# Last pair of expert columns exchanged, dense blocks first in the output sum, its products kept in written order

## The chip, the cores and the metric

The kernel runs on one core of one Trainium2 chip. The metric is the device time of one execution in microseconds; the median of the runs of the kernel before is 2418.31 us. TensorE is called PE (PEld is its loading of weights), VectorE DVE, ScalarE ACT, GpSimd POOL and SyncE SP. Everything is float32 at the edges; many products run in pieces of the type fp32r, which the kernel makes itself by splitting a number into a rounded part ("hi") and the rest ("lo").

## The reference

A layer of a diffusion backbone for 256 latent and 256 context tokens of width 2048: a modulated norm, one input projection, a bidirectional mLSTM and a differential attention, a gated merge, an output projection, and then the part that matters here, a retrieval of experts (PEER):

```python
def peer(h, w_pq, sub_keys, expert_u, expert_v):
    ...
    top_s, pos = lax.top_k(cand_s, P_TOPK)
    idx = jnp.take_along_axis(cand_i, pos, axis=-1)
    g = jax.nn.softmax(top_s, axis=-1)
    ...
        act = jax.nn.gelu(jnp.einsum('td,ted->te', hx, expert_u[ix]).astype(jnp.float32), approximate=False)
        return jnp.einsum('te,ted->td', (gx * act).astype(h.dtype), expert_v[ix])
```

Each of the 256 tokens picks 8 x 16 of 16384 experts; an expert is a row of `expert_u` (2048 numbers, gives its activation) and a row of `expert_v` (2048 numbers, added to the output with gate times activation).

## The kernel before, in words

**The sum over expert columns.** The kernel does not gather `expert_u`; it multiplies all of it. The 16384 experts are 128 columns (i1) of 128 experts. The loop over `i1` at the end of `build` takes two columns at a time ("a pair"). `u_pair` (L80, `mp_`) makes 4 x 16 products for a pair from four pieces of `expert_u`, which the generator `pieces` names in order, `load` (L104) brings in by SP's queue into three buffers, and ACT (L120) and DVE or POOL (L123) split into hi and lo. DVE sums the halves (L1507), ACT takes the gelu (L1508), and ACT's queue stores the activations to the table `ag_dram` in HBM (L1512). Beside this loop `plan` runs in small steps: it finds the top experts, builds the gates of every expert and token (`gate_map`, stored to `ag_dram` by `map_out`, L1235, on SP's queue), and sorts the experts that are in use into lists (`lists`).

**Dense and listed columns.** The last two columns, 126 and 127 (N_LIST = 126), are not listed: their activations stay on chip in `act_tail`, are multiplied by `gate_tail` (L1513), and all their 128 experts enter the output sum ("dense"). For the other 126 columns `lists` makes 99 blocks of 128 experts: 37 blocks for both token tiles (BOTH), 14 for one tile (7 and 7), and 48 for 32 tokens each, of which four make one group. `idxV` and `idxG` hold the row numbers of a block in `expert_v` and `ag_dram`.

**The output sum.** `ITEMS` sets its order: a block, or a group of four. `stage_rows` brings a block's 128 rows of `expert_v` (128x2048, 1 MB) into `vraw`: a dense block by SP's queue, a listed one by an indirect gather on POOL's queue (L1429, `gather`). `vraw` tiles hold two blocks, and there are four of them, which share their place with the tiles `gates` of `gate_map`. `stage_gates` gathers a block's gates and activations (`ag`, 128x512 for BOTH, else 128x256) from `ag_dram`, so it needs all stores of the table. `weights_of` multiplies the two (L1466; L1463 for a group) and, but for groups, splits the product into the halves l (or d for a dense block; L1450 on ACT, L1451 on DVE). `split` does the same for rows (L1442 on ACT, L1444 on DVE). The products go to eight banks of PSUM, `out_acc[t][c]` (v00 to v13: token tile t, 512 columns c). `v_part` (L1525) makes three products (hi-hi, lo-hi, hi-lo) for each bank of a half, with all 128 columns of the array: 24 for a BOTH or dense block, 12 for a block of one tile, 1104 in all. `v_groups` (L1539) multiplies a group unsplit: block j of the four writes 32 output partitions from 32 j, so that it uses 32 columns of the array:

```python
        for c in range(4):
            for j, (raw, ins) in enumerate(parts):
                mm(out_acc[t][c][32 * j:32 * j + 32, :], lhsT=ins[t], rhs=raw[:, c * 512:(c + 1) * 512],
```

These 16 products appear as 32 matmuls in the trace (384 for twelve groups). `next_item` and `fetch_gates` fetch ahead: eight blocks of rows, 8 and 4 `ag` tiles.

**What sets the order.** A framework puts instructions of each engine in an order that it finds by its own estimate of times, unless `tc.keep_in_program_order` (as in `mp_`) keeps an instruction in the order in which the code issues it. In the kernel before the products of `u_pair` are kept so, those of the output sum aren't. All gathers of POOL are kept in their order. After the first N_FIRST = 5 items an `If` (L1562) handles blocks for which there was no room in the lists (none here); behind it `fin` tiles (four of 1 MB: the final norm's weight, a modulation row, the residual) are loaded.

Of the kernel before, what the change touches and what calls it, by code (L numbers as in the profile page):

```python
# [25 lines left out]
OP = mybir.AluOpType  # L26
# [4 lines left out]
P = 128  # L31
# [21 lines left out]
N_LIST = P - 2  # L53
CAPS = (6,) * 8 + (7, 7, 37)
# [5 lines left out]
BOTH, DENSE = 10, 11  # L60


def spread(*groups):
    return [x for _, _, x in sorted(((i + 0.5) / len(g), j, x) for j, g in enumerate(groups) for i, x in enumerate(g))]

ITEMS = [[(BOTH, i)] for i in range(3)] + [[(DENSE, i)] for i in range(N_LIST, P)] + spread(
    [[(4 * t + j, i) for j in range(4)] for i in range(6) for t in range(2)],
    [[(BOTH, i)] for i in range(3, CAPS[BOTH])],  # L70
    [[(8 + n % 2, n // 2)] for n in range(11)]) + [[(9, 5)], [(8, 6)], [(9, 6)]]


def build(tc, a, dump=None):
    nc = tc.nc
    mm = nc.tensor.matmul


    def mp_(*args, **kw):
        tc.keep_in_program_order(mm(*args, **kw))  # L80
# [45 lines left out]
    def pieces():  # L126
        first = [BLOCKS.index(b) for b in FIRST]
        for kp in range(8):
            for i in first:
                yield a["w_in"][i, kp]  # L130
        for i in range(len(BLOCKS)):
            for kp in range(8 if i not in first else 0):
                yield a["w_in"][i, kp]
        for blk in range(4):
            for kp in range(8):
                yield a["w_pb" if kp < 4 else "w_pa"][blk, kp % 4]
        for n in ("w_out", "w_pq"):
            for i in range(32):
                yield a[n][i // 8, i % 8]
        for i in range(2 * P):  # L140
            yield a["expert_u"][i // 2, i % 2]

    ahead = []
    todo = pieces()
# [263 lines left out]
    for k in range(KT):  # L408
# [7 lines left out]
        for kp in range(4):  # L416
            w = load(a["w_mod1"][k, kp], stx, MOD_BUFS)
            for k4 in range(4):
                mm(ps[32 * k4:32 * k4 + 32, 0:T], lhsT=s1[:, 4 * kp + k4, :], rhs=w[:, k4 * T:(k4 + 1) * T],
                   start=kp == 0, stop=kp == 3, skip_group_check=True)  # L420
# [670 lines left out]
    act_tail = tkr.tile([P, P - N_LIST, T], F32, name="act_tail")  # L1091
    gate_tail = tkr.tile([P, P - N_LIST, T], F32, name="gate_tail")
# [314 lines left out]
    n = P - N_LIST + 1  # L1407
# [61 lines left out]

    FIRST_OF = [sum(len(x) for x in ITEMS[:n]) for n in range(len(ITEMS) + 1)]  # L1470
    rows_in = []
    gates_in = []
    staged = [0, 0]


    AG = 8, 4
    USES = [[sum(k != DENSE and len(TILES[k]) == w for k, _ in x) for w in (1, 2)] for x in ITEMS]

    def fetch_gates(n):
        while staged[1] < len(ITEMS) and all(sum(u[w] for u in USES[n:staged[1] + 1]) <= AG[w] for w in range(2)):  # L1480
            gates_in.append([stage_gates(*b) for b in ITEMS[staged[1]]])
            staged[1] += 1

# [9 lines left out]

    back.append(plan())
    pump(1)
    for i1 in range(0, P, 2):
        if i1 == N_LIST:

            drain()
            vst = tc.alloc_tile_pool(name="vst", bufs=1, side="right", reuse_waits="tile")  # L1500
        pss = u_pair(i1, 1.05)
        if i1 == N_LIST:
            (raw0, ins0), = next_item(0)
            hl0 = split(raw0[:, 0:1024])
        act = act_tail if i1 == N_LIST else gm.tile([P, 2, T], F32, name="act", tag="act", bufs=2)
        for e, ps in enumerate(pss):
            nc.vector.reduce_sum(act[:, e], ps.rearrange("p s t -> p t s"), axis=AX.X)  # L1507
        nc.scalar.activation(act, act, AF.Gelu)  # L1508
        if i1 < N_LIST:
            rows = ag_dram[i1 * P:(i1 + 2) * P].rearrange("(i p) (t c) -> p i t c", p=P, t=2)  # L1510
            for t in range(2):
                nc.scalar.dma_start(rows[:, :, t, 0:P], act[:, :, t * P:(t + 1) * P])  # L1512
    nc.vector.tensor_tensor(act_tail, act_tail, gate_tail, op=OP.mult)  # L1513
    psS.release()
    psG.release()
    h2p.release()
# [3 lines left out]
    out_acc = [[psV.tile([P, 512], F32, name=f"v{t}{c}") for c in range(4)] for t in range(2)]  # L1520

    def v_part(hl, ins, t, hf_, first=False, last=False, cs=(0, 1)):
        for i, (sa, sb) in enumerate(PASS):
            for c in cs:
                mm(out_acc[t][hf_ * 2 + c], lhsT=ins[sa], rhs=hl[sb][:, c * 512:(c + 1) * 512],  # L1525
                   start=first and i == 0, stop=last and i == 2, skip_group_check=True)

    def v_block(n, raw, ins, hl=None):
        for hf_ in range(2):
# [6 lines left out]
    def v_groups(t, parts):  # L1536
        for c in range(4):
            for j, (raw, ins) in enumerate(parts):
                mm(out_acc[t][c][32 * j:32 * j + 32, :], lhsT=ins[t], rhs=raw[:, c * 512:(c + 1) * 512],  # L1539
                   start=False, stop=False, skip_group_check=True)  # L1540

    def v_item(n):
        parts = next_item(n)
# [3 lines left out]
            v_block(n, *parts[0])  # L1547

    v_block(0, raw0, ins0, hl0)
    N_FIRST = 3 + P - N_LIST  # L1550
    for n in range(1, N_FIRST):
        v_item(n)

# [8 lines left out]
    with tc.If(rest > 0):  # L1562
        with tc.For_i(0, N_LIST, 1) as i:
            col_ = av.tile([P, 1], F32, name="ocol", bufs=1)
            nc.sync.dma_start(col_, over_dram[:, bass.ds(i, 1)])
            for t in range(2):
                ag = av.tile([P, 2 * P], F32, name="oag", bufs=1)
                nc.sync.dma_start(ag, ag_dram[bass.ds(i * P, P), 2 * t * P:2 * (t + 1) * P])
                w = av.tile([P, P], F32, name="ow", bufs=1)
                nc.vector.scalar_tensor_tensor(w, ag[:, 0:P], col_, ag[:, P:2 * P], op0=OP.mult, op1=OP.mult)  # L1570
                ins = halves(w, P, "o", 1, av)
                for c in range(4):
                    raw = av.tile([P, 512], F32, name="oraw", bufs=1)
                    nc.sync.dma_start(raw, FULL[bass.ds(i * P, P), c * 512:(c + 1) * 512])
                    hl = halves(raw, 512, "r", 1, av)
# [131 lines left out]
```

## Time and profile before

| | |
|---|---|
| runs | 2418.4, 2416.95, 2418.31 us; median 2418.31 |
| profiled execution | 2422.88 us, of which the span from the first to the last instruction is 2421.2 us |
| PE busy | 2326.2 us (96% of the span) |
| DVE, ACT, POOL busy | 1542.8, 1140.5, 894.1 us |
| moved | 571.04 MB, mean 236 GB/s |
| granted clock of TensorE | 0.985 of full speed in the mean |

The span has some 2023 us up to the last product of the expert columns, and then the output sum and the end. PE is busy nearly all the time, but a busy PE need not be at its peak: a matmul with 32 of 128 columns of the array counts as much as one with all of them. So the time of each kind of product is read from the time between starts in a stretch, and the DMA's share and rate beside it.

### The profile page before, as it was taken

How to read it: one execution, taken by the hardware profiler on the slowest of the kernel's cores; microseconds unless marked ns; L12 is line 12 of the kernel's file. 1: busy time of each engine (PE TensorE's matmuls, PEld its weight loads, DVE VectorE, ACT ScalarE, POOL GpSimd, SP SyncE). 2: the span in 40 equal slices, each digit the busy share in tenths (PEclk: the TensorE clock that was granted, in tenths of full speed). 3: DMA queues.
4: the chain of work that ended last, by engine and by line, in shares of the span. 5: the costliest groups of instructions: out<-in, count | busy, mean ns of one | idle time of the engine just before them, and what ended most of it. 6: DMA issues, size and time to landing. Idle time of an engine off the chain costs nothing. (4 is left out here: it accounts for less than half of the span.)

```text
span 2421.2 us, 38180 instructions
## 1 busy us (share of the span) xinstructions
PE 2326.2 (96%) x14434; PEld 1971.9 (81%) x14434; DVE 1542.8 (64%) x2808; ACT 1140.5 (47%) x1913; POOL 894.1 (37%) x910
## 2 busy tenths in 40 slices
PE   6999999999999999989999989999999998999996
PEld 3679989998898999779888878887889887665663
DVE  3357874669766768564788976675665545444445
ACT  3231322244548544444446766794358643333333
POOL 2132201236533200000145564672237524656552
PEclk9999999999999999999999999999999999999998
DMA  9969855875536788755565567788765568998884
GB/s 383 347 201 321 318 192 180 287 214 165 153 115 189 239 281 272 244 197 184 165 200 173 174 183 222 218 219 238 216 191 170 163 213 293 385 368 321 344 337 158
DMA packets 235899, 571.04 MB, mean 236 GB/s; under 512 B 85138, under 2 KB 118723, under 8 KB 221248
## 3 DMA queue, kind: packets, MB, share of 16 engines
q1 hardware_dynamic: 153744, 338.29, 43.7%
q0 software_dynamic: 47120, 212.72, 24.7%
q10 hardware_dynamic: 34848, 17.57, 2.5%
q8 instruction: 113, 1.85, 0.3%
q14 instruction: 74, 0.61, 0.1%
HBM read 524.33 MB, written 38.93 MB: 233 GB/s over the span
## 5 line engine op out<-in xcount | busy, mean ns | idle before, releaser
L120 ACT CAST hi<-raw 128x1024 fp32r<-128x1024 f32 x528 | 552.4, 1048 | 794.0 <-PE acc L275 257.3
L123 DVE TENSOR_TENSOR lo<-raw,hi 128x1024 fp32r<-128x1024 f32 x465 | 590.2, 1272 | 328.8 <-ACT hi L120 323.0
L80 PE MATMUL s<-h,hi 128*128 128x512 f32 x2048 | 740.4, 403 | 1.0 <-ACT hi L120 1.0
L80 PE MATMUL s<-h,lo 128*128 128x256 f32 x2048 | 579.5, 283 | 20.8 <-POOL lo L123 11.5
L80 PEld LDWEIGHTS s<-h,hi 128*128 128x128 f32 x2048 | 388.2, 190 | 88.7 <-ACT hi L120 1.7
L275 PE MATMUL acc<-hL,hi 128*128 128x256 f32 x2048 | 420.5, 285 | 0.0
L80 PEld LDWEIGHTS s<-h,lo 128*128 128x128 f32 x2048 | 390.0, 190 | 28.7 <-POOL lo L123 14.2
L275 PEld LDWEIGHTS acc<-hL,hi 128*128 128x128 f32 x2048 | 339.4, 192 | 4.2 <-issue 3.9
L275 PE MATMUL acc<-hL,lo 128*128 128x256 f32 x1024 | 291.3, 285 | 3.9 <-DVE lo L123 3.9
L123 POOL TENSOR_TENSOR lo<-raw,hi 128x1024 fp32r<-128x1024 f32 x63 | 152.4, 2419 | 275.5 <-ACT hi L120 261.7
L1525 PE MATMUL v<-hi,l 128*128 128x512 f32 x704 | 197.7, 398 | 8.7 <-ACT l L1450 8.6
L1444 DVE TENSOR_TENSOR lo<-vraw,hi 128x1024 fp32r<-128x1024 f32 x106 | 129.2, 1234 | 118.1 <-ACT hi L1442 116.3
L275 PEld LDWEIGHTS acc<-hL,lo 128*128 128x128 f32 x1024 | 196.2, 192 | 5.9 <-DVE lo L123 4.9
L104 POOL DMA_DIRECT2D raw<-w_mod x128 | 67.9, 531 | 305.9 <-DVE raw L508 284.7
L508 DVE SCALAR_TENSOR_TENSOR raw<-raw,cr 128x1024 f32<-128x1024 f32 x128 | 154.9, 1221 | 36.9 <-DMA raw<-w_mod 21.4
L1223 POOL TENSOR_SCALAR o<-iota,i1T,gT 128x128 f32<-128x128 f32 x128 | 140.8, 1107 | 94.5 <-PE g L80 50.3
L1442 ACT CAST hi<-vraw 128x1024 fp32r<-128x1024 f32 x106 | 108.7, 1046 | 138.4 <-PE v L1525 134.0
L1525 PEld LDWEIGHTS v<-hi,l 128*128 128x128 f32 x704 | 132.5, 190 | 49.5 <-issue 10.6
L1429 POOL DMA_INDIRECT vraw<-expert_v,idxV x99 | 105.7, 1068 | 105.4 <-DVE l L1451 31.5
L275 PE MATMUL acc<-hC,hi 128*128 128x256 f32 x512 | 134.0, 283 | 0.0
L1507 DVE TENSOR_REDUCE act<-s 128x256 f32<-128x512 f32 x126 | 86.4, 686 | 58.1 <-PE s L80 52.8
L1429 POOL DMA_INDIRECT ag<-ag_dram,idxG x99 | 102.6, 1036 | 47.3 <-issue 26.2
(406 smaller groups left out, 3971.9 us busy)
## 6 DMA issues: line engine op xcount, KB each, us to landing
raw<-expert_u SPq DMA_DIRECT2D x256, 512.0 KB, 4.1
raw<-w_in SPq DMA_DIRECT2D x176, 512.0 KB, 4.5
raw<-w_mod POOLq DMA_DIRECT2D x128, 512.0 KB, 5.3
raw<-w_mod SPq DMA_DIRECT2D x64, 512.0 KB, 7.4
raw<-w_out SPq DMA_DIRECT2D x32, 512.0 KB, 3.6
raw<-w_pq SPq DMA_DIRECT2D x32, 512.0 KB, 3.3
ag_dram<-gates SPq DMA_DIRECT2D x32, 512.0 KB, 6.7
ag_dram<-act ACTq DMA_DIRECT2D x126, 128.0 KB, 4.0
```

The lines of the kernel that those rows point to most:

```text
L80: tc.keep_in_program_order(mm(*args, **kw))
L104: d = queue.dma_start(r, src)
L120: nc.scalar.copy(h, r)
L123: (nc.vector if shared[0] else nc.gpsimd).tensor_tensor(l, r, h.bitcast(F32), op=OP.subtract)
L275: mm(acc[c][:, g * T:(g + 1) * T], lhsT=hl[sb][:, k2 * 512 + c * P:k2 * 512 + (c + 1) * P], rhs=rhs(sa, g, k), start=first and k2 == 0 and ...
L508: product = nc.vector.scalar_tensor_tensor(r, r, 1.0, cr, op0=OP.mult, op1=OP.mult, accum_out=part[:, h, i:i + 1])
L1223: (nc.gpsimd if i % 2 else nc.vector).tensor_scalar(o2[:, i, 0:width], iota[:, 0:width], cols[:, i:i + 1], factor[:, i:i + 1], op0=OP.is_e ...
L1429: tc.keep_in_program_order(nc.gpsimd.indirect_dma_start(out=out, out_offset=None, in_=src, in_offset=bass.IndirectOffsetOnAxis(ap=idx[:, b ...
L1442: nc.scalar.copy(h, raw)
L1444: nc.vector.tensor_tensor(l, raw, h.bitcast(F32), op=OP.subtract)
L1507: nc.vector.reduce_sum(act[:, e], ps.rearrange("p s t -> p t s"), axis=AX.X)
L1525: mm(out_acc[t][hf_ * 2 + c], lhsT=ins[sa], rhs=hl[sb][:, c * 512:(c + 1) * 512], start=first and i == 0, stop=last and i == 2, skip_group ...
```

## The change

Three things change. `PAIRS` exchanges the last two pairs of columns: 122, then 126 (the dense pair), then 124. The pieces of `expert_u` follow this order, and `act_tail` is multiplied by `gate_tail` as soon as the dense pair's gelu is done. `ITEMS` puts the two dense blocks first, then two BOTH blocks; the third goes to the spread list. The gates for items behind the first are now fetched only when the second item is called for (`fetch_gates`), since they need the stores of pair 124; the `If` stands behind four items. And the products of `v_part` and `v_groups` go through `mp_`, so that PE has them in the order in which the code issues them.

```diff
-ITEMS = [[(BOTH, i)] for i in range(3)] + [[(DENSE, i)] for i in range(N_LIST, P)] + spread(
+ITEMS = [[(DENSE, i)] for i in range(N_LIST, P)] + [[(BOTH, i)] for i in range(2)] + spread(
     [[(4 * t + j, i) for j in range(4)] for i in range(6) for t in range(2)],
-    [[(BOTH, i)] for i in range(3, CAPS[BOTH])],
+    [[(BOTH, i)] for i in range(2, CAPS[BOTH])],
     [[(8 + n % 2, n // 2)] for n in range(11)]) + [[(9, 5)], [(8, 6)], [(9, 6)]]
+
+PAIRS = list(range(0, P - 4, 2)) + [P - 2, P - 4]
...
-        for i in range(2 * P):
-            yield a["expert_u"][i // 2, i % 2]
+        for i in PAIRS:
+            for j in range(4):
+                yield a["expert_u"][i + j // 2, j % 2]
...
-        while staged[1] < len(ITEMS) and all(sum(u[w] for u in USES[n:staged[1] + 1]) <= AG[w] for w in range(2)):
+        while staged[1] < (len(ITEMS) if n else 1) and all(sum(u[w] for u in USES[n:staged[1] + 1]) <= AG[w] for w in range(2)):
...
-    for i1 in range(0, P, 2):
-        if i1 == N_LIST:
+    for i1 in PAIRS:
+        if i1 == PAIRS[-1]:
...
-        if i1 == N_LIST:
+        if i1 == PAIRS[-1]:
             (raw0, ins0), = next_item(0)
...
-    nc.vector.tensor_tensor(act_tail, act_tail, gate_tail, op=OP.mult)
+        else:
+            nc.vector.tensor_tensor(act_tail, act_tail, gate_tail, op=OP.mult)
...
-                mm(out_acc[t][hf_ * 2 + c], lhsT=ins[sa], rhs=hl[sb][:, c * 512:(c + 1) * 512],
-                   start=first and i == 0, stop=last and i == 2, skip_group_check=True)
+                mp_(out_acc[t][hf_ * 2 + c], lhsT=ins[sa], rhs=hl[sb][:, c * 512:(c + 1) * 512],
+                    start=first and i == 0, stop=last and i == 2, skip_group_check=True)
...
-                mm(out_acc[t][c][32 * j:32 * j + 32, :], lhsT=ins[t], rhs=raw[:, c * 512:(c + 1) * 512],
-                   start=False, stop=False, skip_group_check=True)
+                mp_(out_acc[t][c][32 * j:32 * j + 32, :], lhsT=ins[t], rhs=raw[:, c * 512:(c + 1) * 512],
+                    start=False, stop=False, skip_group_check=True)
...
-    N_FIRST = 3 + P - N_LIST
+    N_FIRST = 4
```

What this does to the order of instructions, at three places. In the rows the line comes first (the changed program has other line numbers: L82 is `mp_`, L106 `load`, L1238 `map_out`, L1426 `stage_rows`), then the operation, the tile written and the tiles read.

**PE, the head of the output sum.** Before:

```order
L80 MATMUL s_20497<-h2_15_10177,lo_20479 128x256
L1525 MATMUL v00_20581<-hi_20567,l0_20557 128x512
L1525 MATMUL v01_20582<-hi_20567,l0_20557 128x512
L1525 MATMUL v00_20581<-lo_20569,l0_20557 128x512
L1525 MATMUL v01_20582<-lo_20569,l0_20557 128x512
L1525 MATMUL v02_20583<-hi_20601,l0_20557 128x512
```

Now:

```order
L82 MATMUL s_20495<-h2_15_10177,lo_20477 128x256
L82 MATMUL v00_20556<-hi_20540,d0_20536 128x512
L82 MATMUL v01_20557<-hi_20540,d0_20536 128x512
L82 MATMUL v00_20556<-lo_20542,d0_20536 128x512
L82 MATMUL v01_20557<-lo_20542,d0_20536 128x512
L82 MATMUL v00_20556<-hi_20540,d1_20537 128x512
```

The first products before read l, made from a gathered `ag` tile of a listed block; now they read d, made from `act_tail`, and 48 of them stand ahead of the first that reads an l.

**PE, the second group of four blocks** (w32 are the four blocks' weights, in order of j). Before:

```order
L1539 MATMUL v10_20585<-vraw_21009,w32_21183 32x512
L1539 MATMUL v11_20586<-vraw_21009,w32_21183 32x512
L1525 MATMUL v02_20583<-lo_21166,l0_21138 128x512
...
L1525 MATMUL v13_20588<-hi_21164,l1_21145 128x512
L1539 MATMUL v12_20587<-vraw_21009,w32_21183 32x512
L1539 MATMUL v13_20588<-vraw_21009,w32_21183 32x512
L1539 MATMUL v10_20585<-vraw_21009,w32_21185 32x512
L1539 MATMUL v11_20586<-vraw_21009,w32_21185 32x512
L1539 MATMUL v12_20587<-vraw_21009,w32_21185 32x512
```

Now:

```order
L82 MATMUL v13_20563<-hi_21118,l1_21099 128x512
L82 MATMUL v10_20560<-vraw_20960,w32_21134 32x512
L82 MATMUL v10_20560<-vraw_21009,w32_21136 32x512
L82 MATMUL v10_20560<-vraw_21009,w32_21138 32x512
L82 MATMUL v10_20560<-vraw_21012,w32_21140 32x512
L82 MATMUL v11_20561<-vraw_20960,w32_21134 32x512
L82 MATMUL v11_20561<-vraw_21009,w32_21136 32x512
```

Before, the banks changed and the block stayed, and eight products of another block stood in between; now the four blocks come one after the other for each bank, and the group stands together. Eleven of the twelve groups stood torn by eight products and, for the most part, block by block, like this one; the first had one product early, and its other fifteen stood as the code has them.

**SP, the rows of the dense blocks.** Before, behind all but one of the loads of `expert_u`:

```order
L104 DMA raw_20421<-expert_u 128x1024
L104 DMA raw_20453<-expert_u 128x1024
L1423 DMA vraw_20533<-expert_v 128x2048
L1423 DMA vraw_20536<-expert_v 128x2048
L104 DMA raw_20475<-expert_u 128x1024
```

Now, among the stores of the gates:

```order
L106 DMA raw_16797<-expert_u 128x1024
L1238 DMA ag_dram_83<-gates_15751 128x16x64
L1426 DMA vraw_20528<-expert_v 128x2048 x2
L106 DMA raw_16839<-expert_u 128x1024
L106 DMA raw_16883<-expert_u 128x1024
L1238 DMA ag_dram_83<-gates_15751 128x16x64
```

Both 1 MB loads moved ahead by some 130 places of SP's queue, behind the fifth of the eight stores of the third quarter of the gates. On POOL, three rows of listed blocks are gathered ahead of the first `ag` tile instead of four, and nine `ag` tiles instead of eleven ahead of the rows of the first group.

## Rows read from the trace of the kernel before

**Rows 1.** The page: the span.

```profile
span 2421.2 us, 38180 instructions
```

**Rows 2.** Busy time by stretch: us, five engines, granted clock, DMA share, GB/s.

```profile
2008.00:2023.00 15.00, 14.68 (x84) 12.51 (x82) 7.71 (x8) 6.07 (x7) 5.33 (x5) 1.00 1.02 420
2031.00:2037.00 6.00, 5.72 (x15) 4.53 (x16) 3.00 (x13) 1.52 (x6) 4.76 (x5) 0.55 0.60 174
2070.00:2100.00 30.00, 30.00 (x136) 18.32 (x129) 13.80 (x27) 10.08 (x15) 19.41 (x19) 1.00 1.02 421
2100.00:2150.00 50.00, 50.00 (x200) 32.93 (x199) 22.75 (x46) 16.73 (x25) 32.34 (x31) 1.00 0.98 389
2150.00:2200.00 50.00, 50.00 (x206) 31.07 (x205) 24.13 (x47) 19.21 (x28) 28.38 (x27) 1.00 0.86 331
```

**Rows 3.** Timeline of PE: start, us, line, tiles, count, [idle before <- releaser].

```profile
2022.41 0.28 PE L80 MATMUL s<-h,lo 128*128 128x256 f32 x1
2031.28 1.22 PE L1525 MATMUL v<-hi,l 128*128 128x512 f32 x2 [8.60 <-ACT l L1450]
...
2036.48 0.62 PE L1525 MATMUL v<-hi,l 128*128 128x512 f32 x2
...
2050.42 1.10 PE L1525 MATMUL v<-hi,d 128*128 128x512 f32 x4
2061.89 1.17 PE L1525 MATMUL v<-hi,l 128*128 128x512 f32 x4
2065.79 1.04 PE L1539 MATMUL v<-vraw,w 128*32 128x512 f32 x2
...
2401.94 0.63 PE L1525 MATMUL v<-hi,l 128*128 128x512 f32 x1
```

**Rows 4.** Timelines of POOL, ACT and DVE at the head of the output sum.

```profile
2013.28 1.13 POOL L1429 DMA_INDIRECT vraw<-expert_v,idxV  x1 [0.30 <-issue]
2027.22 0.95 POOL L1429 DMA_INDIRECT ag<-ag_dram,idxG  x1 [12.81 <-SPq L1562]
2028.47 0.95 POOL L1429 DMA_INDIRECT ag<-ag_dram,idxG  x1 [0.30 <-issue]
2012.90 0.94 ACTq L1512 DMA_DIRECT2D ag_dram<-act  x2
2023.56 0.62 ACT L1508 ACTIVATE act_tail<-act_tail 128x512 f32<-128x512 f32 x1
2022.72 0.69 DVE L1507 TENSOR_REDUCE act_tail<-s 128x256 f32<-128x512 f32 x1 [0.64 <-PE s L80]
```

**Rows 5.** The tile `ag_dram`, 1990 to 2060 us: all its DMAs.

```profile
DMA to landing us min/median/max: 2.7/3.6/13.1
```

**Rows 6.** Chain that ended last: start, us, what, number of matmuls.

```profile
2068.89 3.56 PE v L1539 x30
...
2090.32 1.83 PE v L1539 x4
2092.15 2.06 PE v L1525 x8
2094.22 7.06 PE v L1539 x28
2101.27 17.84 PE v L1525 x76
...
2376.59 7.06 PE v L1539 x28
```

**Rows 7.** Timeline of PEld: the first group, then the second.

```profile
2069.28 0.13 PEld L1539 LDWEIGHTS v<-vraw,w 128*32 128x32 f32 x4 [0.30 <-issue]
...
2099.39 0.11 PEld L1539 LDWEIGHTS v<-vraw,w 128*32 128x32 f32 x1 [0.32 <-issue]
```

**Rows 8.** Busy time by stretch while the gates are stored; columns as in rows 2.

```profile
1610.00:1620.00 10.00, 9.51 (x63) 8.40 (x62) 8.38 (x18) 10.00 (x26) 6.51 (x8) 1.00 0.88 246
```

**Rows 9.** Waits from 2062 to 2380 us: total, times, longest.

```profile
POOL vraw L1429 <- PE v L1539: 25.7, 10, 10.5
```

## The prediction

> **What bounds the kernel now.** I read the page first: a span of 2421.2 us [rows 1], around which 1.7 us lie (2422.88 us in this execution). Then I read stretches, since a PE that is busy all the time may still do slow work. The expert columns end at 2022.7 us (2022.41 + 0.28) and the output sum begins at 2031.28 [rows 3]. From 2070 to 2200 PE never idles [rows 2], and the chain that ended last is PE alone up to the last group at 2376.59 [rows 6]. So there the time is PE's, and what a change is worth is the time between starts of its products. Three places matter.
>
> First, the hole of 8.60 us ahead of the output sum [rows 3]. PE waits for l, that for an `ag` gather that POOL could only start at 2027.22 after 12.81 us of waiting [rows 4]. The gather needs all stores of `ag_dram`; the last two were issued from 2012.90 on [rows 4], and one store in this stretch took 13.1 us to land where the median is 3.6 [rows 5]: 2013.4 + 13.1 = 2026.5. The DMA was full then (share 1.02 at 420 GB/s [rows 2]) with four gathered rows and two dense ones. After the hole the granted clock is 0.55 over 6 us [rows 2], a mix of the levels 1.2 and 2.4 GHz: from 2031.28 to 2036.48 twelve products start [rows 3], 0.433 us apart, where 76 take 17.84 us later, 0.235 each [rows 6].
>
> Second, the groups. In the steady part the chain shows a period of 28.8 us: 84 full products (17.84 + 2.06) and one group (1.83 + 7.06 = 8.89 us for 32 matmuls) [rows 6]. But the first group, whose products stand block after block for each bank, takes 3.56 us for 30 [rows 6]. The weight loads tell why: there four loads begin within 0.13 us, then a pause of 0.30, a beat of 0.43 us [rows 7]. In a later group the same beat carries a single load in places [rows 7]. Four blocks use four different quarters of the array's columns, and where they follow each other they run side by side; products of one block must take turns.
>
> Third, the DMA. It moves 421 GB/s at a share of 1.02 from 2070 to 2100, 389 at 0.98 to 2150, then 331 at 0.86 [rows 2]. Here it is no bound, but there is little room.
>
> **The change part by part.**
>
> *Dense blocks first.* After the last product the sum takes 0.69 us (to 2023.41), the gelu 0.62 from 2023.56 on, the two stores 0.94 to issue [rows 4]; with the median landing of 3.6 us [rows 5] the table is complete at 2028.7, as no dense row is in the queue any more. From the first gather to the first product it took 4.06 us (2027.22 [rows 4] to 2031.28 [rows 3]), so the first BOTH block is ready at 2032.8. PE has 48 dense products until then, which took 11.5 us (2050.42 to 2061.89 [rows 3], the `If` within), so until 2034.2: covered, with 1.4 us to spare. If a store lands later, PE waits that much more. Gain: 8.60 us, and the slow clock, 12 x (0.433 - 0.235) = 2.4 us. Sum: **-11.0 us**.
>
> *Pinned products.* Eleven groups fall from 8.89 to 3.56 us [rows 6], 58.6 us; the first loses its early product, 0.98 us (two matmuls from 2065.79 to the next product at 2066.77; 1.04 in its row [rows 3]). Sum: **-59.6 us**. The full products' order changes too, at nothing on PE: 0.235 us each either way, if their halves are ready. What is queued behind a wait on PE is now everything, where the old order could put in something else.
>
> *Dense rows loaded early.* SP issues both 1 MB loads at about 1619 us, among small stores, where the DMA has a share of 0.88 at 246 GB/s and PE already loses 0.49 us in 10 [rows 8]. 2.1 MB at 421 GB/s [rows 2] are 5 us, at 246 GB/s 8.5 us, and the loads of `expert_u` stand behind them in SP's queue. The three buffers give little cover. I take **+4 us**, bounds 0 and 8.
>
> *What is late next: the rows of listed blocks.* A period now needs 19.9 + 3.56 = 23.5 us of PE. It moves eight rows (8 x 1.049 MB), three `ag` tiles of 0.262 MB and five of 0.131: 9.83 MB, 23.3 us at 421 GB/s. So PE and DMA are level. In total: three rows go out early; nine `ag` tiles at 1.25 us each (2027.22 to 2028.47 [rows 4]) occupy POOL from 2028.7 to 2040, so data flow from 2041. From then on 96 rows, 33 and 57 `ag` tiles and four `fin` tiles are 100.7 + 8.7 + 7.5 + 4.2 = 121.0 MB. At 421 GB/s they end at 2041 + 287 = 2328, at 389 at 2041 + 311 = 2352. The products behind the last row, with their waits on DVE, I take from the end of the trace, some 9 us. So the last product ends at 2337 or at 2361; PE alone would end at 2402.6 (2401.94 + 0.63 [rows 3]) - 11.0 - 59.6 = 2332. The DMA gives back 5 to 29 us; I take the middle, **+17 us**. Much of it should fall early, where `fin` (10 us of DMA) now meets the rows of the first groups. POOL's issue is no bound: 186 gathers x 1.25 us = 233 us of some 300. What follows the last product (2402.6 to 2421.2) keeps its instructions: nothing, within 2 us.
>
> *Sum:* 2422.9 - 11.0 - 59.6 + 4 + 17 = 2373.3 us. This execution lies 4.6 us above the median of the runs (2418.3), so the forecast is **2369 us**.
>
> **The rivals.**
>
> *A: the DMA keeps up.* PE sets the end, no loss at 1619: 2418.3 - 70.6 = 2348 us. For it: eight rows of lookahead, 421 GB/s held for 30 us. Against: 389 in the next 50 us, with small `ag` packets between rows.
>
> *B: the DMA sustains less than in its best stretches.* At 358 GB/s the 121.0 MB take 338 us, the last product ends at 2388, and it is 2418.3 - 70.6 + 56 + 4 = 2408 us. Against it stand the 420 and 421 GB/s [rows 2]; for it, that no stretch shows them for 300 us. The figure is that of the Trainium skill (DMA: Bandwidth & Descriptors, Where 436 GB/s comes from), by which the core's half of the HBM, about 358 GB/s, binds transfers from HBM; the trace disagrees over the 30 us.
>
> *C: the groups gain nothing from their order.* The first group may be fast for another reason, say that its rows had long landed. Then only the transition is left: 2418.3 - 11.0 + 4 = 2411 us. Against it: the beat of 0.43 us with one to four loads in it [rows 7], and PE never waits in the torn groups [rows 2]. By the Trainium skill (TensorE: Matmul & The Clock Gate, The mechanism) a weight load overlaps matmuls in flight only if it goes to other rows of the array; all four blocks use all 128 rows, so the order would bring nothing. The trace disagrees: four loads in 0.13 us [rows 7]. This rival holds the case, too, that the change doesn't do what it says.
>
> *D: slower, by blocked gathers.* POOL's queue is in order, and a gather that waits for a `vraw` tile holds all behind it. In the trace ten such waits on a group's products took 25.7 us [rows 9], and the DMA fell to 331 GB/s [rows 2]. Now all four rows of a group come free at its end instead of one after the other. If this keeps the rate at 331 although PE asks for more, the 121.0 MB take 366 us and the last product ends at 2416: 2418.3 - 70.6 + 84 + 4 = 2436 us. It is slower from about 347 GB/s down. Against: at 331 GB/s PE was what POOL waited for, and a faster group frees its rows sooner.
>
> **How the numbers follow.** Forecast 0.60, A 0.17, B 0.08, C 0.10, D 0.05. The range goes from A, 2347, to the forecast's own worst, 2418.3 - 70.6 + 29 + 8 = 2385, and a little further for PE's clock, which may fall again in a wait of several us as it did after the hole [rows 2]: 2390. B, C and D are outside (0.23), but part of C and B lies between their ends and the forecast; with that some 2 in 10 are left out. A measurement can tell about 0.2% (4.8 us) from no change. B, by 10 us, and C, by 7, are still faster; half of a C in which the loss at 1619 is 8 us is the same. Faster 0.91, same 0.04, slower 0.05.
>
> **What would show it.** The twelve groups should each stand in one piece of about 3.6 us in PE's timeline, with four loads to a beat. Between the last product of the columns and the first of the output sum there should be no hole and no slow clock; the reads of d come first. The column loop should end a few us later, with PE idle around 1620 us. The DMA share should be near 1.0 from 2041 us on, with over 390 GB/s, and PE should idle some 10 to 20 us for `vraw` rows, most of it before 2100. The forecast is wrong if groups take 7 us or more, if PE idles over 30 us behind 2041, or if the rate stays near 331 GB/s while PE waits.

## The result, and the profile after

The changed kernel takes 2383.57 us (median; 2381.84 to 2387.03) against 2418.36 us: a ratio of 0.9857, 95% interval 0.9841 to 0.9872. It is faster by 1.4%, inside the range of the prediction and 14.6 us above its forecast of 2369. The profiled execution took 2382.48 us.

The page of the kernel after, its span [rows 1] and the busy time of its engines:

```profile
span 2380.8 us, 38170 instructions
...
PE 2276.5 (96%) x14434; PEld 1954.2 (82%) x14434; DVE 1540.7 (65%) x2808; ACT 1139.7 (48%) x1913; POOL 896.0 (38%) x910
```

Busy time by stretch, columns as in [rows 2]; the second stretch holds the first group, the last two are most of the output sum, and its end:

```profile
2008.00:2023.00 15.00, 15.00 (x78) 12.64 (x77) 8.11 (x9) 7.22 (x9) 1.70 (x2) 1.00 0.53 200
...
2040.00:2060.00 20.00, 14.35 (x60) 6.33 (x59) 2.18 (x2) 1.99 (x2) 9.46 (x10) 0.83 1.01 410
...
2041.00:2330.00 289.00, 270.78 (x1272) 184.51 (x1271) 146.98 (x286) 110.60 (x165) 194.38 (x181) 0.99 0.98 389
2330.00:2366.00 36.00, 27.68 (x116) 17.08 (x114) 22.12 (x27) 12.91 (x22) 8.14 (x7) 0.91 0.46 188
```

The DMA is now full for 289 us, at 389 GB/s, and PE idles 18 us in that time, where before it idled in none of the stretches behind 2070 [rows 2].

PE's timeline: the end of the expert columns, the first, the second and an undisturbed later group (columns as in [rows 3]):

```profile
2016.02 0.28 PE L82 MATMUL s<-h,lo 128*128 128x256 f32 x1
2016.14 0.62 PE L82 MATMUL v<-hi,d 128*128 128x512 f32 x2
...
2027.30 0.62 PE L82 MATMUL v<-hi,l 128*128 128x512 f32 x2
...
2044.99 1.05 PE L82 MATMUL v<-vraw,w 128*32 128x512 f32 x4
2046.75 1.04 PE L82 MATMUL v<-vraw,w 128*32 128x512 f32 x2 [0.70 <-DMA vraw<-expert_v,idxV]
2051.72 5.63 PE L82 MATMUL v<-vraw,w 128*32 128x512 f32 x26 [3.92 <-DMA vraw<-expert_v,idxV]
...
2080.40 1.05 PE L82 MATMUL v<-vraw,w 128*32 128x512 f32 x4
2083.02 1.04 PE L82 MATMUL v<-vraw,w 128*32 128x512 f32 x2 [1.57 <-DMA vraw<-expert_v,idxV]
2085.50 3.62 PE L82 MATMUL v<-vraw,w 128*32 128x512 f32 x26 [1.44 <-DMA vraw<-expert_v,idxV]
...
2236.13 3.64 PE L82 MATMUL v<-vraw,w 128*32 128x512 f32 x32
2239.70 0.72 PE L82 MATMUL v<-hi,l 128*128 128x512 f32 x2
```

The hole of 8.60 us [rows 3] is gone, and the first l (2027.30) comes without a wait. A group whose rows are there takes 3.57 us (2236.13 to 2239.70). The first takes 12.85 (2044.99 to 2057.84) and the second 8.72. Of the 9.3 us that the first takes above 3.57, PE stands idle 4.62 for rows; of the 5.2 of the second, 3.01. In the rest it counts as busy, with products one or two at a time ahead of a row that isn't there yet, and in the first group for a while at half the clock (0.50 from 2050 to 2054 us).

PE's two largest sums of waits from 2016 to 2366 us (total, times, longest):

```profile
PE v L82 <- DVE lo L1447: 13.3, 17, 3.8
PE v L82 <- DMA vraw<-expert_v,idxV: 11.9, 9, 3.9
```

All nine waits for rows lie inside groups. The 17 waits for lo, the half that DVE makes, lie between the other products; three of them, 6.3 us, come behind 2350 us.

The output sum from the last product of the columns to its own last product was 379.9 us and is 349.7. I split it by the starts in PE's timeline: a group from its first product to the next other one, and all other products together. Before, the twelve groups take 102.2 us, the others 268.4 and the hole the rest; after, 68.8 and 280.5. Twelve groups of 3.57 us would be 42.8. So the groups, with the waits in them, cost 26 us more than they would with their rows there, and the others 12 more than before. The column loop ended 6.4 us earlier in this execution, and what follows the last product took 14.8 instead of 18.6 us: with the 30.2 us of the output sum these are the 40.4 us between the spans.

### The profile page after: what moved, and what is told of

Same layout as the page of the kernel before. It is cut to its first block, busy times and chain, and to the rows that moved or that the text cites. A ratio compares the mean times of both kernels' runs of the same rounds, so it can differ in the third digit from the quotient of the medians.

```text
span 2380.8 us, 38170 instructions
## 1 busy us (share of the span) xinstructions
PE 2276.5 (96%) x14434; PEld 1954.2 (82%) x14434; DVE 1540.7 (65%) x2808; ACT 1139.7 (48%) x1913; POOL 896.0 (38%) x910
## 5 line engine op out<-in xcount | busy, mean ns | idle before, releaser
L82 PE MATMUL s<-h,hi 128*128 128x512 f32 x2048 | 737.0, 402 | 1.0 <-ACT hi L122 1.0
L82 PE MATMUL s<-h,lo 128*128 128x256 f32 x2048 | 577.8, 282 | 18.7 <-DVE lo L125 9.6
L82 PEld LDWEIGHTS s<-h,hi 128*128 128x128 f32 x2048 | 386.4, 189 | 88.1 <-ACT hi L122 1.8
L82 PEld LDWEIGHTS s<-h,lo 128*128 128x128 f32 x2048 | 388.3, 190 | 27.4 <-DVE lo L125 15.1
L82 PE MATMUL v<-hi,l 128*128 128x512 f32 x704 | 198.1, 398 | 1.6 <-ACT hi L1445 1.4
L106 POOL DMA_DIRECT2D raw<-w_mod x128 | 67.9, 531 | 306.9 <-DVE raw L511 285.6
L82 PEld LDWEIGHTS v<-hi,l 128*128 128x128 f32 x704 | 132.0, 189 | 43.7 <-ACT hi L1445 13.0
L1432 POOL DMA_INDIRECT vraw<-expert_v,idxV x99 | 115.0, 1161 | 43.2 <-issue 21.8
L82 PE MATMUL v<-lo,l 128*128 128x512 f32 x352 | 113.9, 403 | 13.4 <-DVE lo L1447 13.3
```

Of the source, the lines that this page charges most:

```text
L106: d = queue.dma_start(r, src)
L1432: tc.keep_in_program_order(nc.gpsimd.indirect_dma_start(out=out, out_offset=None, in_=src, in_offset=bass.IndirectOffsetOnAxis(ap=idx[:, b ...
```

## The experiments

All ratios are to runs of the kernel before that were taken beside each kernel; its median there lay between 2415.9 and 2420.0 us, so times and ratios need not fall in the same order. "Groups" and "others" are the two sums just named, from one profiled execution each, which need not be a middling one (e1's took 2389.7 us, e7's 2370.9, e9's 2371.5, e11's 2378.8); a wait ahead of a group's first product counts with the others. "Early loss" is what the starts of products between 2040 and 2100 us lie apart above 0.235 us for a full product and 0.111 us for a matmul of a group (in before, e2 and e4 it holds the slow groups too; a wait that begins ahead of 2040 is not in it).

| kernel | us | ratio, 95% interval | groups | others | early loss |
|---|---|---|---|---|---|
| before | 2418.36 | 1 | 102.2 | 268.4 | 6.2 |
| after | 2383.57 | 0.9857 (0.9841 to 0.9872) | 68.8 | 280.5 | 18.0 |
| e1_pin_only | 2383.21 | 0.9837 (0.9802 to 0.9872) | 58.4 | 285.7 | 8.9 |
| e2_order_only | 2421.03 | 1.0014 (0.9997 to 1.0031) | 111.9 | 269.2 | 20.2 |
| e3_half_rows | 2379.10 | 0.9826 (0.9789 to 0.9863) | 62.9 | 277.5 | 14.9 |
| e4_block_order | 2416.87 | 0.9989 (0.9976 to 1.0001) | 105.5 | 277.3 | 16.6 |
| e5_fin_early | 2376.27 | 0.9820 (0.9803 to 0.9837) | 62.1 | 277.4 | 11.1 |
| e6_rows_early | 2385.90 | 0.9866 (0.9848 to 0.9884) | 53.6 | 290.2 | 19.0 |
| e7_fin_rows_early | 2378.47 | 0.9833 (0.9818 to 0.9848) | 45.9 | 290.4 | 11.9 |
| e8_tail | 2388.09 | 0.9876 (0.9858 to 0.9895) | 67.3 | 278.4 | 17.8 |
| e9_row_by_row | 2377.18 | 0.9838 (0.9815 to 0.9861) | 55.9 | 283.7 | 7.7 |
| e10_row_by_row_fin | 2374.32 | 0.9823 (0.9802 to 0.9843) | 61.1 | 280.5 | 4.6 |
| e11_six_rows | 2383.84 | 0.9864 (0.9842 to 0.9886) | 57.1 | 293.6 | 9.6 |
| e12_half_early | 2366.18 | 0.9783 (0.9765 to 0.9801) | 43.3 | 285.6 | 1.0 |

**The two parts of the change alone.** e1 is the kernel before with the pinning, e2 the kernel after without it:

```diff
-                mm(out_acc[t][hf_ * 2 + c], lhsT=ins[sa], rhs=hl[sb][:, c * 512:(c + 1) * 512],
+                mp_(out_acc[t][hf_ * 2 + c], lhsT=ins[sa], rhs=hl[sb][:, c * 512:(c + 1) * 512],
...
-                mm(out_acc[t][c][32 * j:32 * j + 32, :], lhsT=ins[t], rhs=raw[:, c * 512:(c + 1) * 512],
+                mp_(out_acc[t][c][32 * j:32 * j + 32, :], lhsT=ins[t], rhs=raw[:, c * 512:(c + 1) * 512],
```

> The kernel before with the pinned products alone (order of columns and blocks as before). Theory: the gain of the groups hangs on the pinning alone, and the bytes of the DMA give most of the rest back. Each of the twelve groups takes about 3.6 us instead of 8.9, the hole of some 9 us ahead of the output sum stays, the DMA share is near 1.0 behind it; with the hole the DMA gets some 10 us for its rows, so that the end is set by the DMA again: 2384 to 2396 us. Rival, the gain needs the new order of blocks: groups stay at 7 us or more and the time over 2408 us.

> The kernel after without the pinning. Theory: only the transition is gained, -11 us, and the small loss from the early dense rows, +2 to +4: 2407 to 2412 us, groups torn and near 8.9 us, no PE wait for rows to speak of. Rival, the order of blocks is what brought the gain: 2380 to 2390 us.

e1 came out 0.8 us under the range of the theory, with its groups whole and its hole in place; e2 missed its range by 9 us: the new order alone gains nothing. PE's timeline of e2 has no hole, and then this at the first group:

```profile
2017.76 0.28 PE L82 MATMUL s<-h,lo 128*128 128x256 f32 x1
2017.88 0.62 PE L1529 MATMUL v<-hi,d 128*128 128x512 f32 x2
...
2047.54 1.05 PE L1543 MATMUL v<-vraw,w 128*32 128x512 f32 x4
2050.15 2.77 PE L1543 MATMUL v<-vraw,w 128*32 128x512 f32 x16 [1.56 <-DMA vraw<-expert_v,idxV]
2055.11 3.62 PE L1543 MATMUL v<-vraw,w 128*32 128x512 f32 x10 [2.19 <-DMA vraw<-expert_v,idxV]
2061.24 2.07 PE L1529 MATMUL v<-hi,l 128*128 128x512 f32 x4 [2.51 <-ACT hi L1445]
```

From 2047.54 to 2061.24 it takes 13.7 us, where the same 30 matmuls took 3.56 before [rows 6]: 10.1 us are lost, a little after the hole's 8.6 were gained: 3.75 of them are waits for rows, 2.51 one for the next block's hi. And e1 still has its hole (7.61 us), its first group is whole and waits for nothing (3.57 us), and its time is that of both parts together. So the hole was also the time in which the first rows landed; without it PE stands a little later, for them. The whole measured gain is the pinning's.

**Why a pinned group is fast.** e4 keeps the pinning and turns the two loops round:

```diff
-        for c in range(4):
-            for j, (raw, ins) in enumerate(parts):
+        for j, (raw, ins) in enumerate(parts):
+            for c in range(4):
```

> The kernel after, still pinned, but with the products of a group block after block (the four banks of one block, then the next block). Theory: four blocks run side by side only where they follow each other, so a group takes 7 to 9 us again, 12 x (3.4 to 5.3) = 41 to 64 us more of PE, of which the some 40 us that the DMA gives back cover a part: 2395 to 2412 us. Rival, a group is fast as long as no other block's products stand within it: 3.6 us a group and 2380 to 2388 us.

Measured: 2416.87 us, 4.9 above the upper end: of 62.6 us more for the groups (12 x 5.22) only 29 were covered. A group in e4's timeline of PE, and of PEld within it:

```profile
2253.45 8.86 PE L82 MATMUL v<-vraw,w 128*32 128x512 f32 x32
2262.24 0.72 PE L82 MATMUL v<-hi,l 128*128 128x512 f32 x2
```

```profile
2253.90 0.11 PEld L82 LDWEIGHTS v<-vraw,w 128*32 128x32 f32 x1 [0.32 <-issue]
2254.33 0.11 PEld L82 LDWEIGHTS v<-vraw,w 128*32 128x32 f32 x1 [0.32 <-issue]
...
2255.19 0.14 PEld L82 LDWEIGHTS v<-vraw,w 128*32 128x32 f32 x3 [0.32 <-issue]
```

The same in the kernel after, for the group at 2236.13:

```profile
2236.58 0.13 PEld L82 LDWEIGHTS v<-vraw,w 128*32 128x32 f32 x4 [0.30 <-issue]
2237.01 0.13 PEld L82 LDWEIGHTS v<-vraw,w 128*32 128x32 f32 x4 [0.30 <-issue]
```

Both beat every 0.43 us; in e4 one to three loads go in a beat, 32 in 19 beats, and in the kernel after four. All twelve groups of e4 take 8.79 us. So neither the pinning itself nor the absence of foreign products makes a group fast, but that its four blocks follow each other. With the pinning in block order the whole change would have come to a ratio of 0.9989 (0.9976 to 1.0001).

**Is it the bytes?** e3 lets each gather of a listed block bring 1024 numbers instead of 2048:

```diff
-            gather(raw, FULL, idxV, BASE[kind] + i)
+            gather(raw[:, 0:1024], HALF, idxV, BASE[kind] + i)
...
-                hl = split(raw[:, hf_ * 1024:(hf_ + 1) * 1024])
+                o = hf_ * 1024 if ITEMS[n][0][0] == DENSE else 0
+                hl = split(raw[:, o:o + 1024])
```

> The kernel after with half of each listed row: every gather of a listed block brings 1024 numbers of a row instead of 2048, and the products of the second half use the first half's numbers again, so half of those rows of expert_v is left out; the count of gathers, products and splits is that of the kernel after. Theory, the bytes of the DMA gave back some 40 us: 50 of 121 MB less, the DMA is no bound any more, PE sets the end: 2340 to 2352 us, PE's waits for rows under 3 us. Rival, POOL's queue in order (gathers that wait for a free tile hold others behind them, 1.25 us for each issue): as many gathers as before, so 2372 to 2384 us.

My theory, that bytes alone took back the 40 us, fell: 2379.10 us, in the rival's range. Three stretches of e3 by busy time (columns as above):

```profile
2060.00:2080.00 20.00, 18.19 (x74) 13.22 (x72) 11.48 (x24) 7.48 (x12) 14.96 (x15) 1.00 0.90 320
2080.00:2100.00 20.00, 17.20 (x79) 10.29 (x80) 9.63 (x23) 7.88 (x13) 11.79 (x11) 1.00 0.48 157
...
2150.00:2200.00 50.00, 50.00 (x248) 36.14 (x247) 28.29 (x57) 20.88 (x32) 35.90 (x33) 1.00 0.65 217
```

From 2150 to 2200 PE never waits any more, with a DMA share of 0.65. But between 2080 and 2100 PE idles 2.8 us while the DMA is half empty: there the rows had been asked for late. POOL's timeline of e3 at that place (the second group's rows):

```profile
2068.02 0.96 POOL L1433 DMA_INDIRECT vraw<-expert_v,idxV  x1 [0.30 <-issue]
2069.28 0.94 POOL L1433 DMA_INDIRECT vraw<-expert_v,idxV  x1 [0.30 <-issue]
```

From 2063 to 2086 it issues one gather behind the other, mostly 1.25 us apart; then it stands 5.46 us for a place that PE has to give free. And behind 2340 e3's products lie 9 us further apart than 0.235 us each, as those of the kernel after do.

**The early loss.** The next kernels look for its cause. e5 changes one number, and with it the place of the If and of the four 1 MB loads:

```diff
-    N_FIRST = 4
+    N_FIRST = 2
```

> The kernel after with the If and with it the four 1 MB loads of the last tiles (fin) behind two items of the output sum instead of four, so that they go out at about 2027 us, where the DMA has room, and not at 2040, where the rows of the first groups are asked for. In the kernel after, and also with half rows, PE loses 15 to 18 us between 2040 and 2100. Theory, these loads stand in the way of the first rows: the loss there falls to 8 to 12 us and the time to 2372 to 2379 us. Rival, the rows are late because POOL asks for them late (nine gate tiles first, rows only for free places): the loss stays at 15 to 18 us and the time at 2380 to 2387.

The loads went out at 2028.54 instead of 2039.23 us. The second group then stood without a wait (3.57 us, 8.72 in the kernel after), the first still took 13.96, and the time fell to 2376.27 us, in the range of the theory. e6 asks for rows earlier:

```diff
-    [[(BOTH, i)] for i in range(2)] + spread(
+    [[(BOTH, 0)]] + [[(j, 0) for j in range(4)]] + spread(
...
+        if i1 == PAIRS[-3]:
+            drain()
+            fetch_rows(0)
```

> The kernel after with the rows of the first eight blocks asked for three pairs of columns earlier, and the first group of four put right behind the first listed block, so that its four rows are among these eight: six listed rows go out early instead of three, and before the last pairs' products are done. Theory that POOL asks late: the first group no longer waits, three rows (3.1 MB, 8 us at 389 GB/s) leave the full stretch, the loss between 2040 and 2100 falls from 18 to 8 to 10 us, 2372 to 2378 us. Rival, the last tiles' loads alone stand in the way: the next group waits instead, 2380 to 2386 us.

> Both of the two edits before it (last tiles' loads behind two items; six listed rows early, the first group among them). If bytes that move out of the full stretch are what counts, 7.3 MB or 19 us at 389 GB/s leave it: 2362 to 2370 us, loss between 2040 and 2100 under 5 us. If the depth of eight rows limits, the second and third groups still wait: 2371 to 2378 us.

e6 gained nothing (2385.90 us, in the rival's range), in two ways. Six rows in the middle of the column loop hold up the loads of `expert_u`:

```profile
1980.00:2000.00 20.00, 18.54 (x104) 15.61 (x104) 6.67 (x7) 6.41 (x7) 8.75 (x7) 1.00 0.96 363
2000.00:2020.00 20.00, 15.96 (x79) 12.99 (x79) 10.33 (x12) 7.53 (x9) 2.36 (x1) 0.91 0.56 215
```

PE loses 5.5 us in these 40. And the first group, which now comes early, stands at 3.82 us, but the second waits instead: 6.30 us for rows ahead of it, and then it takes 12.89. e7, with the early loads in addition, ends at 2378.47 us, half a us above its second range and where e5 does: the two edits don't add. Not for the reason given, though: its groups take 45.9 us in all, so their rows are nearly always there; the others take 290.4, and PE waits 20 us for lo and hi.

e9 asks for the rows one by one, so that the three places left over take three rows of the first group, from 2001.59 us on, when the loads of `expert_u` are nearly done, and at the start asks for fewer gates ahead of the next rows; e10 adds the early loads of e5:

```diff
-        while staged[0] < len(ITEMS) and (FIRST_OF[staged[0] + 1] - 1) // 2 * 2 - 7 < FIRST_OF[n]:
-            rows_in.append([stage_rows(*b) for b in ITEMS[staged[0]]])
+        while staged[0] < len(BLOCKS_) and staged[0] // 2 * 2 - 7 < FIRST_OF[n]:
+            rows_in.append(stage_rows(*BLOCKS_[staged[0]]))
...
-        while staged[1] < (len(ITEMS) if n else 1) and all(sum(u[w] for u in USES[n:staged[1] + 1]) <= AG[w] for w in range(2)):
+        while staged[1] < min(upto, (1, 6)[n] if n < 2 else len(ITEMS)) and all(sum(u[w] for u in USES[n:staged[1] + 1]) <= AG[w] for w in range(2)):
```

> The kernel after with rows staged one by one instead of item by item: the three places that the first group could not use are taken by three of its four rows, asked for with the first listed rows at about 2003 us, six instead of three; and at the start POOL asks for the gates of the first six items only (seven tiles, not nine) before the next rows. Order of blocks and place of the If as in the kernel after. Theory, the loss of 18 us between 2040 and 2100 is the time that the first rows are asked for too late: 3.1 MB (8 us at 389 GB/s) leave the full stretch and the first group no longer waits: loss there 6 to 10 us, 2372 to 2378 us. Rival, as when the rows were asked for much earlier, the wait only moves to the next group, behind the 4 MB of the last tiles: 2381 to 2387 us.

> Rows one by one as in the run before it and the last tiles' loads behind two items instead of four. If the two causes of the early loss add, the loss between 2040 and 2100 falls under 5 us: 2364 to 2371 us. If they are one and the same (room in the DMA before 2060, which one of them uses up), 2372 to 2378 us as with the early loads alone.

e9 did as the theory had it: first group 3.57 us, early loss 7.7, 2377.18 us. In e10 the early loss falls to 4.6, as if the causes added, but the time, 2374.32 us, lies in the second range, and ahead of 2040 there is a new loss: with rows and last tiles in the queues, the first gates land late, and PE has a wait of the old kind, ahead of the first listed block:

```profile
2031.66 1.22 PE L82 MATMUL v<-hi,l 128*128 128x512 f32 x2 [5.28 <-ACT l L1453]
```

It is the fastest complete kernel by its median, but its interval holds all of e5's. e5 is faster than the kernel after by some 0.4% with one number changed: its interval ends at 0.9837, that of the kernel after begins at 0.9841.

e11 tries the depth of the look-ahead, six blocks instead of eight:

```diff
-        while staged[0] < len(ITEMS) and (FIRST_OF[staged[0] + 1] - 1) // 2 * 2 - 7 < FIRST_OF[n]:
+        while staged[0] < len(ITEMS) and (FIRST_OF[staged[0] + 1] - 1) // 2 * 2 - 5 < FIRST_OF[n]:
```

> The kernel after with rows staged six blocks ahead instead of eight (one pair of places fewer in use). Bytes and their order stay. If bytes set the pace from 2100 to 2330 us, the DMA stays full with less to choose from, 2383 to 2392 us, its share at 0.97 or more. If the depth of the look-ahead does, rows come later by some 5 us for each group and the DMA idles more: 2400 to 2430 us, share under 0.93.

The time doesn't change: 2383.84 us, share 0.99 to 1.00 in each stretch from 2100 to 2300 (ahead of the first group there is now a wait of 10.75 us for rows, which the table has with the others, and not in the early loss). So with full rows the depth isn't what limits the middle; the DMA, full throughout, fits. e12 is e10 with half rows:

> Half of each listed row, as in the third run (half of those rows of expert_v left out, the first half used twice), on top of rows one by one and the early loads of the last tiles. In the run with half rows alone POOL issued some 50 gathers one behind the other from 2040 to 2110 us, and groups waited 5 us for rows that it had asked for late, with the DMA far from full; from 2150 on PE had no wait. Theory, that waiting is the late asking at the start: with three more rows asked for at 2003 and the last tiles out of the way it goes, 12 to 15 us of the 15 us loss between 2040 and 2100: 2362 to 2368 us, and what then is left above PE's own sum is the end behind 2340. Rival, the eight places and POOL's 1.25 us for each gather hold the rows back throughout, whatever their bytes: 2371 to 2378 us, as without half rows.

2366.18 us, in the theory's range. All twelve groups take 3.57 to 3.86 us, and the waits of PE over its output sum (total, times, longest) are only these:

```profile
PE v L82 <- DVE lo L1448: 19.4, 19, 4.4
PE v L82 <- ACT hi L1446: 0.2, 1, 0.2
```

So rows that come late, by bytes or by asking, are behind the groups' 26 us. What is left is not the end alone, as the theory had it: 12.5 of the 19.4 us for lo fall ahead of 2330 us. The chain that ended last in e12 tells what such a wait hangs on:

```profile
2205.97 3.19 DMA ag<-ag_dram,idxG
...
2209.25 0.49 DVE w L1470 x2
2209.74 1.15 DVE lo L1448
...
2210.93 11.95 PE v L82 x66
```

Ahead of its split DVE stands for a block's `ag` tile, and POOL has issued that gather as the seventh of a row that begins at 2197.38. So with half the bytes it is POOL's pace over rows and gates that is left in the middle, and not DVE by itself. With slow groups that pace was enough: in e4 PE waits for nothing between 2068 and 2388 us.

**The end.** e8 keeps the splits of the last three blocks ahead of the residual, on DVE and ACT:

```diff
-        nc.scalar.copy(h, raw)
+        keep(nc.scalar.copy(h, raw))
...
-    for c in range(4):
-        residual(0, c)
+    h2 = [half(r2, 0)]
+    h0.append(half(r0, 1))
```

> The kernel after with the splits of the last three blocks kept ahead of the residual on DVE and ACT, by program order. In the kernel after PE waits 6.3 us for lo behind 2350 us while DVE works on the residual. Theory: these waits are order on DVE, not rows: the last product comes 4 to 6 us sooner, some of which the residual behind it gives back: 2377 to 2382 us. Rival, the residual is only put off and the end is the same: 2383 to 2386 us with 4 us more behind the last product.

Nothing was gained, as the rival had it, and the time lies 2 us above its range: 2388.09 us. PE's timeline of e8 in place of the waits for lo:

```profile
2360.47 0.79 PE L82 MATMUL v<-hi,l 128*128 128x512 f32 x1 [2.90 <-ACT hi L1445]
2362.22 0.79 PE L82 MATMUL v<-lo,l 128*128 128x512 f32 x1 [0.96 <-DVE lo L1447]
...
2365.37 0.63 PE L82 MATMUL v<-hi,l 128*128 128x512 f32 x1
```

The sixth split waits for one of three buffers. The last product falls at 2365.37 as in the kernel after, though the columns of this execution ended 3.5 us later, so the output sum is 3.5 us shorter (346.2 for 349.7); but what follows it takes 20.1 us instead of 14.8, as the residual is put off.

## Why the prediction was right, and where it was off

*Dense blocks first, -11.0 us.* Right at its place: no hole, clock 1.00, the l in time. Wrong as a term of a sum: e2 shows that nothing of it arrives. The prediction let the loads of the last tiles "meet the rows of the first groups", but counted that in one term for the whole DMA and let the -11.0 stand beside it. The hole and the first rows were two ends of one wait.

*Pinned products, -59.6 us.* Right for the groups. e12, with all rows there, has 43.3 us for them where before had 102.2: 58.9 less. Not right for the full products, whose order the prediction put "at nothing on PE ... if their halves are ready": the halves aren't always. PE waits 13.3 us for lo in the kernel after, where before it waited for none up to 2390 us, and 19.4 us in e12, where the groups wait for nothing. Rival C, that the groups gain nothing, falls with e4 against the kernel after: 8.79 or 3.57 us, by the order of the same products. The rule of the Trainium skill (TensorE: Matmul & The Clock Gate, The mechanism), that a load overlaps only where it goes to other rows, taken by itself would have made both alike; all four blocks use all rows.

*Dense rows loaded early, +4 us.* Nothing, the lower bound, by the end: the products of the columns that start at 1607 us in the kernel after have fallen back by 1.8 us by 1638, against the same products of the kernel before, but by 1960 us they have made it up.

*The rows of listed blocks, +17 us, bounds 5 to 29.* The mis-sized step: what is lost above PE's own sum was 40 us, 26 in groups and 12 in the others plus the 2.4 of slow clock that these no longer have. Only the 26, inside the bounds, are shown to be the rows'; the other 14 are largely waits for halves, which e12 has too, there in the middle behind late gates. That the time lies in the range all the same is in part luck: 11 us above this term's upper bound stand against 4 us for the dense rows and 3.8 behind the last product that were not spent. The rate was at the lower of my two values, 389 GB/s, and the last row that PE's chain waits for was there at 2340.7 (ACT takes it up at 2340.73), even earlier than the 2352 worked out; the very last, which nothing waited for, was asked for at 2341.25 and took 6.9 us. What failed is "the products behind the last row ... some 9 us" and "POOL's issue is no bound". The chain that ended last in the kernel after shows the first; before, it was PE alone [rows 6]:

```profile
2253.85 1.27 POOL vraw L1432
2255.43 1.05 POOL vraw L1432
2258.04 11.01 DMA ag<-ag_dram,idxG
...
2327.71 12.95 DMA vraw<-expert_v,idxV
2340.73 1.05 ACT hi L1445
2341.81 1.24 DVE lo L1447
2343.09 6.58 PE v L82 x27
...
2356.07 1.21 DVE lo L1447
2357.29 1.70 DVE fin L1604
...
2360.11 2.06 DVE lo L1447
```

Behind the landing at 2340.7 stood 60 products (24 of a BOTH block, 36 of the three single ones), 14.1 us at 0.235, and three waits for lo (1.98, 0.48 and 3.83 us), since DVE does the residual between its splits: with the split itself and products that no longer follow closely, 25.3 us to 2366.0. The 9 us came from a trace in which the last rows had long landed. The second shows in e3, e9 and the chain of e12: POOL's 233 us are spread unevenly. Behind 2021 it issues nine tiles of gates before the first row, then mostly one gather right behind the other, and with half the bytes rows and gates still come late.

*What follows the last product: "nothing, within 2 us".* It was 3.8 us less. It goes with the pinning: 18.6 and 18.7 us in before and e2, 14.7 in e1.

*The other rivals.* A fell: PE idled 18 us. B fell: the Trainium skill's figure (DMA: Bandwidth & Descriptors, Where 436 GB/s comes from), about 358 GB/s, is below the 389 measured over 289 us. D fell: POOL's waits for PE behind 2062 us were 10.9 us, 9.7 of them one wait ahead of the last row's gather, against 25.7 [rows 9], while the rate rose.

*Open.* In six profiled executions with the same columns (after, e2, e3, e4, e5, e8) the last of their products starts between 2016.0 and 2020.9 us; in before and e1 at 2022.4 and 2020.6. The 6.4 us between before and after stood already at 1570 us (the same product starts at 1576.79 and 1570.44), ahead of the place where the dense rows are now loaded (1612.64), so that move has no part in them; where they come from is open. Without them the spans lie 34.0 us apart, near the 34.8 of the medians. No kernel tried the late dense rows alone. How much of the middle's loss with full rows is bytes and how much the place of DVE's splits was not separated either, and no kernel pinned the groups alone and left the full products free.

## What to carry to other kernels

Matmuls that use different parts of the array's columns ran side by side here only where they followed each other (3.57 us a group, or 8.79), so their written order is worth as much as their number; a framework's order may undo it, and a pin restores it. A hole ahead of a stage is also time for the stage's transfers: before counting it as a gain, look for what lands in it. When PE gets faster than its feed, count the feed from the first request, on the queue that issues it, to the last product behind the last landing, not only in bytes; and count what else shares that queue, here the gates.

## What the hardware showed that was not expected

- The DMA held 389 GB/s over 289 us, with 8 KB rows and gates of 1 and 2 KB mixed, by gathers that POOL issued at the closest 1.25 us apart.
- A wait of a few us costs PE more than the wait: 26 matmuls of the first group took 5.63 us behind a wait of 3.92, and 26 of the second 3.62 us behind one of 1.44. The granted clock from 2040 to 2060 us was 0.83, a mix of 2.4 and 1.2 GHz; from 2050 to 2054 it was 0.50, the lower of them.
- Executions of one kernel differ by more than I allowed: the kernel before ran from 2412.9 to 2427.9 us over all series, where I had taken 0.2% as what can be told.
